# Attention in an encoder block: another order of its units, reciprocals turned by a transpose, later casts, and ScalarE's and VectorE's order fixed by the program

## The chip, the cores and the metric

The kernel runs on one core of a Trainium2 chip. TensorE multiplies, VectorE and GpSimd work elementwise, ScalarE copies, casts and evaluates functions, and SyncE (SP) issues most of the DMAs; ScalarE has a DMA queue of its own. The metric is the device time of one execution in microseconds. The kernel before takes 2630.07, the median of three runs (2628.52 to 2633.43). Units are microseconds throughout.

## The reference

One layer of an encoder block, for 1024 tokens of width 1024, in float32:

```
h      = rmsnorm(x) * (1 + scale1) + shift1          # scale, shift, gate from silu(c) @ w_ada
q, k, v, xBC, z, dt, gates = split(h @ w_in)
q, k   = rope(rmsnorm(q)), rope(rmsnorm(k))          # 16 query heads, 4 key/value heads of 64
attn   = softmax(q k^T / 8) v                        # over all 1024 tokens, per head
ssd    = gated_rmsnorm(scan_fwd(xBC, dt) + scan_bwd(xBC, dt) + D * x, z)
merged = sigmoid(g_a) * (attn @ w_attn_out) + sigmoid(g_s) * (ssd @ w_ssd_out)
x      = x + gate1 * (merged @ w_o)
x      = x + gate2 * (relu(h2 @ w1)^2 @ w2)          # h2: x normed and modulated again
```

The change touches the line `attn` and what is computed beside it: a part of `gates`, and the making ready of `attn` for the product with `w_attn_out`.

## The kernel before

**Products of float32.** Every large product is made of three: an operand is split into a high part (a cast to a 32-bit format that TensorE takes in one pass) and a low part (the operand minus the high part), and the products high·high, high·low and low·high are added in PSUM. `split` does this: ScalarE casts, VectorE or GpSimd (`e_lo=G`) subtracts. `gemm_cm` runs a product whose weights are the stationary operand: per tile `i` of 128 columns and half of the tokens, eight steps of three matmuls. It loads and splits the weights of tile `i + 1` (`load_w`: the DMA, the cast `whi`, the remainder `wlo`) when tile `i` begins.

**Attention** (`attn_stream`) goes through 128 units: 16 heads by 8 tiles of 128 queries. Four units are a block: a head and 512 queries.

- `scores(u)`: four matmuls give a tile `pss` of 128 queries by 1024 keys in PSUM (two such tiles); VectorE takes the negated row maximum `nm` (L914); ScalarE takes the exponential into `pf` in SBUF (two tiles), with the row sums into a column of `zall` (L916).
- `turn(u, hf)`: four transposes (L927) turn half of `pf` into a PSUM tile `pst` (two tiles); ScalarE casts it to `ph`, VectorE subtracts for `pl`. There are three tiles of `ph` and of `pl`; each holds one half of the keys for a block.
- `values(b, hf)`: with `v` as the stationary operand, eight matmuls a half into one PSUM tile `pv`, whose upper rows hold the high part of `v` and whose lower rows the low one. After the second half ScalarE copies one part (`ax`), VectorE adds the other (`av`), GpSimd multiplies by the reciprocals of the row sums (`rz`), and SP writes `av` to DRAM.
- The reciprocals: VectorE takes them (`zi`, 128 queries by 4 tiles); a DMA on SP writes them to DRAM query by query (L941), and another reads them back broadcast over 64 partitions (L943).

The loop over units issues scores of unit u + 2, the first `turn` of unit u, a quarter of the values of the block before, the second `turn`. `values` yields four times, once per four matmuls.

**Beside it** runs `beside()`: first the products of six tiles of `gates` (`gates_stream`, 96 steps; ScalarE copies each result to `ost` and writes it from its own DMA queue), then `load_a`: it splits two tiles of `w_attn_out`, and per pair of heads loads `av` back (`araw`) and splits it at once into `ah` and `al`, the operands of the product after attention.

**What sets the order.** `weave` takes the next step of that stream which is less far along, by costs written into the `yield`s: attention counts 2.72 a unit, 128 × 2.72 + 18 = 366.2 in all, and what runs beside counts 6 × 10.4 + 18 = 80.4, of which a step of gates is 0.65. A step that yields `None` isn't ready. Inside `tc.manual_schedule(engines=...)` the engines named keep the order in which the program issues; the others are ordered by the scheduler, which simulates the kernel and gives each engine the order of that simulation. Before, the set `M2` for attention holds TensorE alone:

```
M2 = {mybir.EngineType.PE}
...
        with tc.manual_schedule(engines=M2):
            weave(tc, (attn_stream(), 128 * 2.72 + L0), (beside(), GATES * 10.4 + 18), lead=LEAD2)
```

On the chip every engine takes its instructions in the order given to it, and waits where an operand or a buffer isn't ready. A DMA's issue is an instruction of the engine whose queue it uses.

Of the kernel before, what the change touches and what calls it, by code (L numbers as in the profile page):

```python
# [9 lines left out]
F32 = mybir.dt.float32  # L10
# [8 lines left out]
P = 128  # L19
S = 1024  # L20
D = 1024
NT = S // P
KT = D // P
NH = 16
NKV = 4
HD = 64
# [6 lines left out]
OFF_Z, OFF_DT, OFF_G = 4608, 6656, 6720  # L33
# [20 lines left out]
SC0, SC1 = 26, 3.5  # L54
GATES = 16 - 2 * len(GPOS)
M3 = {mybir.EngineType.PE}
M2 = {mybir.EngineType.PE}
LEAD3 = 400
BIG = 1.5 * 2.0 ** 15
BAR = 1e30  # L60
# [30 lines left out]
def block(ctx: ExitStack, tc: tile.TileContext, ia, out, upto=99, dbg=None):  # L91
    nc = tc.nc
    V, A, G, T = nc.vector, nc.scalar, nc.gpsimd, nc.tensor
    dma = nc.sync.dma_start
    adma = nc.scalar.dma_start
# [71 lines left out]
    def split(hi, lo, src, e_hi=None, e_lo=None):  # L167
        (e_hi or A.copy)(hi, src)  # L168
        tt(e_lo or V, lo, src, hi.bitcast(F32), ALU.subtract)
# [4 lines left out]
    def act_tiles(name, n):  # L174
        return [[[act.tile([P, 512], F32R, name=f"{name}{p}_{k}_{h}", tag="act", bufs=32)
                  for h in range(2)] for k in range(n)] for p in ("h", "l")]

    def load_w(src, shape=(KT, P), e_lo=None):

        raw = wp.tile([P, *shape], F32, name="wraw", tag="wraw")  # L180
        dma(raw, src)
        hi = wp.tile([P, *shape], F32R, name="whi", tag="whi")
        lo = wp.tile([P, *shape], F32R, name="wlo", tag="wlo")
        split(hi, lo, raw, e_lo=e_lo)
        return hi, lo

    def w_cols(w, c0, k0=0):
        return w[k0 * P:(k0 + KT) * P, c0:c0 + P].rearrange("(k p) c -> p k c", p=P)

    def gemm_cm(ps_pool, tag, wsrcs, ahi, alo, evac, bufs=None, pair=False, then=None, e_lo=None, ws=None):  # L190

        ws = ws or {0: load_w(wsrcs[0], e_lo=e_lo)}
        if then:
            then()
        n = len(wsrcs)
        order = [(i, h) for i in range(n) for h in range(2)]
        if pair:
            order[:4] = [(0, 0), (1, 0), (0, 1), (1, 1)]
        for i, half in order:
            if half == 0 and i + 1 < n and i + 1 not in ws:  # L200
                ws[i + 1] = load_w(wsrcs[i + 1], e_lo=e_lo)
            hi, lo = ws[i]
            if 1:
                ps = ps_pool.tile([P, 512], F32, name=tag, tag=tag, bufs=bufs)
                for k in range(KT):
                    T.matmul(ps, hi[:, k], ahi[k][half], start=k == 0, stop=False)  # L206
                    T.matmul(ps, hi[:, k], alo[k][half], start=False, stop=False)  # L207
                    T.matmul(ps, lo[:, k], ahi[k][half], start=False, stop=k == KT - 1)  # L208
                    yield 0.65
                evac(i, half, ps)  # L210


# [44 lines left out]
    with tc.tile_pool(name="p0", bufs=1) as p0, tc.tile_pool(name="ps0", bufs=1, space=PSUM) as ps0:  # L257
# [57 lines left out]
        late = []  # L315
# [101 lines left out]
    with tc.tile_pool(name="p1", bufs=1, reuse_waits="tile") as p1, \  # L417
# [428 lines left out]
    with tc.tile_pool(name="p3k", bufs=1, reuse_waits="tile") as p3k, \  # L846
# [3 lines left out]
        def gates_stream(pool, psp, i0, i1, bufs=2, e_lo=None):  # L850
            def evac(i, half, ps):
                st = pool.tile([P, 512], F32, name="ost", tag="ost", bufs=2)
                A.copy(st, ps)
                adma(gt_d[i0 + i][:, half * 512:(half + 1) * 512], st)

            yield from gemm_cm(psp, "psg", [w_cols(w_in, OFF_G + i * P) for i in range(i0, i1)], hhi, hlo, evac, bufs=bufs, e_lo=e_lo)

        heads = [0]
        w_ahead = {}

        def load_a():

            hi, lo = act_tiles("a", KT)
            for i in range(2):
                w_ahead[i] = load_w(w_cols(w_ao, i * P), e_lo=G)
            yield 2
            for k in range(KT):
                while heads[0] < 2 * k + 2:
                    yield None
                for half in range(2):  # L870
                    raw = p3.tile([P, 512], F32, name="araw", tag="araw", bufs=2)
                    dma(raw, av_d[k][:, half * 512:(half + 1) * 512])
                    split(hi[k][half], lo[k][half], raw, e_lo=G)
                yield 2
            w_ahead["a"] = hi, lo

# [4 lines left out]
        def attn_stream():  # L881
# [19 lines left out]
            pfs, phs, pls = {}, {}, {}  # L901

            def scores(u):
                h, t = divmod(u, NT)
                q1 = qs[h]
                k1, k2, _ = kv[h // 4]
                ps = ps3.tile([P, S], F32, name="pss", tag="pss", bufs=2)
                ts = slice(t * P, (t + 1) * P)
                for n in range(2):
                    T.matmul(ps[:, n * 512:(n + 1) * 512], q1[:, ts], k1[:, n * 512:(n + 1) * 512], start=True, stop=False)  # L910
                for n in range(2):
                    T.matmul(ps[:, n * 512:(n + 1) * 512], q1[:, ts], k2[:, n * 512:(n + 1) * 512], start=False, stop=True)  # L912
                nm = p3.tile([P, 1], F32, name="nm", tag="nm", bufs=4)
                V.tensor_reduce(out=nm, in_=ps, axis=AX.X, op=ALU.max, negate=True)  # L914
                pfs[u] = p3.tile([P, S], F32, name="pf", tag="pf", bufs=2)
                A.activation(pfs[u], ps, AF.Exp, bias=nm, accum_out=zall[:, u:u + 1])  # L916

# [13 lines left out]
            pvs, rzs = {}, {}  # L931

            def values(b, hf):

                h = b // 2
                v1 = kv[h // 4][2]
                if hf == 0:
                    zi = p3.tile([P, 4], F32, name="zi", tag="zi", bufs=2)
                    V.reciprocal(zi, zall[:, 4 * b:4 * b + 4])
                    row = rz_d[h:h + 1, (b % 2) * 512:(b % 2 + 1) * 512]  # L940
                    dma(row.rearrange("a (t p) -> p (a t)", p=P), zi)  # L941
                    rzs[b] = p3.tile([HD, 512], F32, name="rz", tag="rz", bufs=2)
                    dma(rzs[b], rz_d[h, (b % 2) * 512:(b % 2 + 1) * 512].partition_broadcast(HD))  # L943
                    pvs[b] = ps3.tile([P, 512], F32, name="pv", tag="pv", bufs=1)
                pv, ph, pl = pvs[b], phs.pop((b, hf)), pls.pop((b, hf))
                for k in range(4):
                    kt = hf * 4 + k
                    if kt == 0:
                        T.matmul(pv, v1[:, 0], ph[:, 0], start=True, stop=False)
                    T.matmul(pv[:HD], v1[:, kt, 0:HD], pl[:, k], start=False, stop=False)  # L950
                    if kt:
                        T.matmul(pv, v1[:, kt], ph[:, k], start=False, stop=kt == NT - 1)
                    if k == 1:
                        yield 0.92
                if hf == 1:
                    ax = p3.tile([HD, 512], F32, name="ax", tag="ax", bufs=1)
                    A.copy(ax, pv[HD:])
                    av = p3.tile([HD, 512], F32, name="av", tag="av", bufs=2)
                    tt(V, av, ax, pv[:HD], ALU.add)
                    tt(G, av, av, rzs.pop(b), ALU.mult)  # L960
                    dma(av_d[h // 2][(h % 2) * HD:(h % 2 + 1) * HD, (b % 2) * 512:(b % 2 + 1) * 512], av)
                    heads[0] = (b + 1) // 2
                yield 0.92

            def all_values(b):
                for hf in range(2):
# [27 lines left out]

# [723 lines left out]
```

## Time and profile before

| what | value |
|---|---|
| median of three runs | 2630.07 |
| profiled execution: time, span | 2632.16, 2630.4 |
| mean granted clock of TensorE | 0.973 |
| busy: TensorE, weight loads, VectorE, ScalarE, GpSimd | 2427.9, 1933.0, 1851.1, 1135.3, 1119.9 |
| first and last row maximum of attention | 791.5, 1288.5 |
| last value matmul begins; product after attention begins | 1300.8, 1301.0 |
| TensorE busy in 784 to 1304: transposes, scores, values, gates | 161.6, 173.1, 209.1, 116.7 |
| VectorE there: row maxima, `pl` | 156.6, 166.8 |
| ScalarE there: exponentials, `ph` | 142.7, 143.6 |

The profile is that of one execution; its time is 1.8 above its span and 2.1 above the median. Matmuls overlap in the array, so the sum of their lengths is more than the time they hold TensorE; their distance from start to start is what counts. In a line of the timeline the first numbers are start and length, then engine, line of the code, operation, result `<-` operands and shape; the brackets hold how long the engine had been idle and what ended that. `PEld` is TensorE's weight load, `ACTq` and `SPq` are DMA issues of ScalarE's and SP's queues. L154 and L168 are the lines of the helpers for elementwise operations and casts, so their instructions are told apart by tiles. In the list of waits stand total, times and longest.

### The profile page before, as it was taken

To read this page: it belongs to the slowest core of one execution; us is meant where nothing else is said; L and a number is where in the kernel's file an instruction comes from. 1 tells how busy PE (TensorE), PEld (TensorE's weight loads), DVE (VectorE), ACT (ScalarE), POOL (GpSimd) and SP (SyncE) were. 2 spreads that over 40 slices of the span, in tenths; PEclk is the share of its full clock that TensorE was granted. 3 is DMA by queue.
4 is the path that set the end of the run, shared out by engine and by line. 5 is a ranking of instruction groups with operands and counts; after the bars stand their busy time and mean duration, and the time that the engine had idled before them with its cause. 6 is when DMAs were issued, how large, how long until landed. Compare 5 with 4: busy or idle time off the path is not lost.

```text
span 2630.4 us, 32563 instructions
## 1 busy us (share of the span) xinstructions
PE 2427.9 (92%) x11291; PEld 1933.0 (73%) x11291; DVE 1851.1 (70%) x2203; ACT 1135.3 (43%) x1964; POOL 1119.9 (43%) x828
## 2 busy tenths in 40 slices
PE   5999999999988999887789989999998999899995
PEld 4898777878776677665567767777776888688884
DVE  5756347777776777656567888646569888767889
ACT  5455423444446666665423444444232222264441
POOL 3210117777760111121146656614017765633356
PEclk9999999999999999989999999999899999899998
DMA  7554741333353222221166666466415544764432
GB/s 262 175 156 129 251 145 60 96 106 103 115 180 92 74 61 65 67 69 41 49 205 199 212 201 185 142 212 204 140 61 172 176 152 146 249 192 143 143 96 96
DMA packets 298293, 369.69 MB, mean 141 GB/s; under 512 B 50953, under 2 KB 179569, under 8 KB 298129
## 3 DMA queue, kind: packets, MB, share of 16 engines
q1 hardware_dynamic: 227953, 292.63, 36.2%
q10 hardware_dynamic: 70176, 74.99, 8.6%
q8 instruction: 89, 1.46, 0.3%
q14 instruction: 75, 0.61, 0.1%
HBM read 251.33 MB, written 116.20 MB: 140 GB/s over the span
## 4 chain that ended last, share of the span: by engine, by line
PE 38%; DMA 8%; DVE 6%; issue 3%; POOL 2%; ACT 1%; SPq 0%; DVEq 0%; ACTq 0%; POOLq 0%
PE pp L1323 4%; PE pp L1325 4%; PE pp L1324 4%; PE p L1665 3%; PE p L1666 3%; PE p L1664 3%; DMA rz<-zi 2%; PE psy L1150 2%; PE psg L206 2%; PE pso L1124 2%; DVE o L154 2%; PE psg L207 2%; PE psg L208 2%; DVE ac L154 1%; PE pso L1370 1%
## 5 line engine op out<-in xcount | busy, mean ns | idle before, releaser
L914 DVE TENSOR_REDUCE nm<-pss 128x1 f32<-128x1024 f32 x128 | 156.6, 1224 | 121.3 <-PE pss L912 119.6
L927 PE MATMUL pst<-masks,pf 128*128 128x128 f32 x1024 | 161.6, 281 | 59.7 <-DVE pl L154 59.6
L927 PEld LDWEIGHTS pst<-masks,pf 128*128 128x128 f32 x1024 | 119.8, 143 | 127.8 <-DVE pl L154 51.9
L380 PE MATMUL psq<-twl,hh 128*128 128x400 f32 (+1 forms) x512 | 192.8, 378 | 7.7 <-DVE twl L154 5.9
L1665 PE MATMUL p<-o,o 128*128 128x512 f32 x448 | 179.9, 402 | 19.0 <-DVE o L154 19.0
L154 DVE TENSOR_TENSOR pl<-pst,ph 128x512 fp32r<-128x512 f32 x256 | 166.8, 681 | 43.1 <-ACT ph L168 43.1
L379 PE MATMUL psq<-twh,hh 128*128 128x400 f32 (+1 forms) x512 | 191.7, 380 | 3.4 <-ACT qkvr L512 1.3
L381 PE MATMUL psq<-twh,hl 128*128 128x400 f32 (+1 forms) x512 | 191.5, 376 | 0.5 <-DVE hl L154 0.5
L916 ACT ACTIVATE pf<-pss,nm 128x1024 f32<-128x1024 f32 x128 | 142.7, 1115 | 108.3 <-PE pst L927 103.0
L154 POOL TENSOR_TENSOR av<-av,rz 64x512 f32<-64x512 f32 x32 | 41.0, 1282 | 339.9 <-DVE av L154 332.7
L1664 PE MATMUL p<-o,o 128*128 128x512 f32 x448 | 177.5, 400 | 8.7 <-ACT o L168 6.8
L1666 PE MATMUL p<-o,o 128*128 128x512 f32 x448 | 177.5, 398 | 0.0
L154 POOL TENSOR_TENSOR sl<-sl 128x512 f32<-128x512 f32 x64 | 95.1, 1491 | 175.6 <-DVE o L154 84.3
L713 DVE SCALAR_TENSOR_TENSOR cacc<-pad,cwT,cacc 128x1024 f32<-128x1024 f32 x96 | 159.5, 1691 | 0.4
L168 ACT CAST ph<-pst 128x512 fp32r<-128x512 f32 x256 | 143.6, 586 | 32.9 <-PE pst L927 21.2
L168 ACT CAST o<-ar 128x512 fp32r<-128x512 f32 x112 | 69.8, 624 | 175.8 <-PE p L1666 160.9
L154 DVE TENSOR_TENSOR o<-ar,o 128x512 fp32r<-128x512 f32 x112 | 107.9, 964 | 48.6 <-ACT o L168 48.4
L168 ACT CAST wop<-ws 128x512 fp32r<-128x512 f32 x132 | 81.5, 622 | 130.6 <-PE pp L1325 69.3
L154 POOL TENSOR_TENSOR wop<-ws,wop 128x512 fp32r<-128x512 f32 x68 | 121.5, 1800 | 20.8 <-ACT wop L168 20.6
L1665 PEld LDWEIGHTS p<-o,o 128*128 128x128 f32 x448 | 86.5, 193 | 41.5 <-DVE o L154 23.7
L380 PEld LDWEIGHTS psq<-twl,hh 128*128 128x128 f32 x512 | 98.2, 192 | 20.0 <-DVE twl L154 7.5
L154 DVE TENSOR_TENSOR wop<-r,wop 128x512 fp32r<-128x512 f32 x89 | 97.7, 1098 | 20.5 <-ACT wop L168 20.2
(414 smaller groups left out, 7230.7 us busy)
## 6 DMA issues: line engine op xcount, KB each, us to landing
ar<-r SPq DMA_DIRECT2D x112, 256.0 KB
wada<-in_w_ada_dram SPq DMA_DIRECT2D x48, 512.0 KB
r<-in_w_in_dram SPq DMA_DIRECT2D x34, 512.0 KB
r<-in_w_mlp_dram SPq DMA_DIRECT2D x32, 512.0 KB
r<-as SPq DMA_DIRECT2D x64, 256.0 KB
sl<-in_w_mlp_dram SPq DMA_DIRECT2D x64, 256.0 KB
r<-ro ACTq DMA_DIRECT2D x48, 256.0 KB
xb<-cst ACTq DMA_DIRECT2D x20, 512.0 KB
```

Of the source, the lines that this page charges most:

```text
L154: e.tensor_tensor(out=o, in0=a, in1=b, op=op)
L168: (e_hi or A.copy)(hi, src)
L379: T.matmul(o, hhi[k][half][:, sl], hi[:, k % 2, :n], start=k == 0, stop=False)
L380: T.matmul(o, hhi[k][half][:, sl], lo[:, k % 2, :n], start=False, stop=False)
L381: T.matmul(o, hlo[k][half][:, sl], hi[:, k % 2, :n], start=False, stop=k == KT - 1)
L713: V.scalar_tensor_tensor(out=acc, in0=pad[:, k:k + S], scalar=cwT[:, 24 * k + i:24 * k + i + 1], in1=acc, op0=ALU.mult, op1=ALU.add)
L914: V.tensor_reduce(out=nm, in_=ps, axis=AX.X, op=ALU.max, negate=True)
L916: A.activation(pfs[u], ps, AF.Exp, bias=nm, accum_out=zall[:, u:u + 1])
L927: T.transpose(pt[:, k], pf[:, (hf * 4 + k) * P:(hf * 4 + k + 1) * P], ident)
L1664: T.matmul(pss[t], a[:, 0, sl], b[:, 0], start=k == 0, stop=False)
L1665: T.matmul(pss[t], a[:, 0, sl], b[:, 1], start=False, stop=False)
L1666: T.matmul(pss[t], a[:, 1, sl], b[:, 0], start=False, stop=k == KR - 1)
```

## The change

- `M2` gets ScalarE and VectorE besides TensorE: in attention their instructions keep the program's order, ScalarE's DMA issues with them.
- The exponential leaves `scores` and becomes `weights(u)`. A unit now issues: both `turn`s of unit u with values between them, scores and row maximum of unit u + 2, `sums` in every fourth unit, then the exponential of unit u + 1.
- Values are yielded as 8, 4 and 4 matmuls, so the four units of a block get 8, 4, 4 and none.
- The reciprocals are taken at the start of the block's first unit; `sums` turns them by a transpose on TensorE (into a `pst` tile), ScalarE copies the four rows to `zr` and writes them from its own queue; SP reads them back broadcast as before.
- `gemm_cm` with `late=5` loads the next weights when a tile begins, and splits them after the sixth step of its first half (`raw_w` is the load alone). `load_a` loads both tiles of `w_attn_out` first and splits them later; of `av` it loads both halves of a pair of heads, and splits them when attention is three units further.

```diff
-M2 = {mybir.EngineType.PE}
+M2 = {mybir.EngineType.PE, mybir.EngineType.Activation, mybir.EngineType.DVE}
...
-    def load_w(src, shape=(KT, P), e_lo=None):
-
+    def raw_w(src, shape=(KT, P)):
         raw = wp.tile([P, *shape], F32, name="wraw", tag="wraw")
         dma(raw, src)
+        return raw
+
+    def load_w(src, shape=(KT, P), e_lo=None, raw=None):
+
+        raw = raw_w(src, shape) if raw is None else raw
...
             if half == 0 and i + 1 < n and i + 1 not in ws:
-                ws[i + 1] = load_w(wsrcs[i + 1], e_lo=e_lo)
+                if late is None:
+                    ws[i + 1] = load_w(wsrcs[i + 1], e_lo=e_lo)
+                else:
+                    raws[i + 1] = raw_w(wsrcs[i + 1])
...
                     yield 0.65
+                    if k == late and i + 1 in raws:
+                        ws[i + 1] = load_w(None, e_lo=e_lo, raw=raws.pop(i + 1))
...
+            raws = [raw_w(w_cols(w_ao, i * P)) for i in range(2)]
             for i in range(2):
-                w_ahead[i] = load_w(w_cols(w_ao, i * P), e_lo=G)
-            yield 2
+                yield 2
+                w_ahead[i] = load_w(None, e_lo=G, raw=raws[i])
             for k in range(KT):
                 while heads[0] < 2 * k + 2:
                     yield None
+                raws = [p3.tile([P, 512], F32, name="araw", tag="araw", bufs=2) for half in range(2)]
                 for half in range(2):
-                    raw = p3.tile([P, 512], F32, name="araw", tag="araw", bufs=2)
-                    dma(raw, av_d[k][:, half * 512:(half + 1) * 512])
-                    split(hi[k][half], lo[k][half], raw, e_lo=G)
+                    dma(raws[half], av_d[k][:, half * 512:(half + 1) * 512])
+                u0 = units[0]
+                while units[0] < min(u0 + 3, NH * NT + 3):
+                    yield None
+                for half in range(2):
+                    split(hi[k][half], lo[k][half], raws[half], e_lo=G)
...
                 V.tensor_reduce(out=nm, in_=ps, axis=AX.X, op=ALU.max, negate=True)
+                sms[u] = ps, nm
+
+            def weights(u):
+                ps, nm = sms.pop(u)
                 pfs[u] = p3.tile([P, S], F32, name="pf", tag="pf", bufs=2)
                 A.activation(pfs[u], ps, AF.Exp, bias=nm, accum_out=zall[:, u:u + 1])
...
+            def sums(b):
+
+                pz = ps3.tile([P, 4, P], F32, name="pst", tag="pst", bufs=2)
+                T.transpose(pz[0:4, 0], zis.pop(b), ident)
+                zr = p3.tile([4, P], F32, name="zr", tag="zr", bufs=1)
+                A.copy(zr, pz[0:4, 0])
+                row = rz_d[b // 2, (b % 2) * 512:(b % 2 + 1) * 512]
+                adma(row.rearrange("(t p) -> t p", p=P), zr)
+                rzs[b] = p3.tile([HD, 512], F32, name="rz", tag="rz", bufs=2)
+                dma(rzs[b], row.partition_broadcast(HD))
...
-                    zi = p3.tile([P, 4], F32, name="zi", tag="zi", bufs=2)
-                    V.reciprocal(zi, zall[:, 4 * b:4 * b + 4])
-                    row = rz_d[h:h + 1, (b % 2) * 512:(b % 2 + 1) * 512]
-                    dma(row.rearrange("a (t p) -> p (a t)", p=P), zi)
-                    rzs[b] = p3.tile([HD, 512], F32, name="rz", tag="rz", bufs=2)
-                    dma(rzs[b], rz_d[h, (b % 2) * 512:(b % 2 + 1) * 512].partition_broadcast(HD))
...
-                    if k == 1:
+                    if hf == 1 and k == 1:
                         yield 0.92
...
-                yield 0.92
+                yield 0.92 if hf else 1.84
...
-            scores(0)
-            yield 0.92
-            scores(1)
-            yield 0.92
+            for u in range(2):
+                scores(u)
+                yield 0.92
+            weights(0)
             pvq = iter(())
             for u in range(NU + 4):
+                units[0] = u
                 if u % NT == 4 and 1 < u // NT + 1 < NH:
                     load_head(u // NT + 1)
-                if u + 2 < NU:
-                    scores(u + 2)
-                    yield 0.92
+                b = u // 4 - 1
+                if u % 4 == 0 and u:
+                    zis[b] = p3.tile([P, 4], F32, name="zi", tag="zi", bufs=2)
+                    V.reciprocal(zis[b], zall[:, 4 * b:4 * b + 4])
                 for hf in range(2):
                     if u < NU:
                         turn(u, hf)
                         yield 0.44
                     if hf == 0:
                         c = next(pvq, None)
                         if c:
                             yield c
+                if u + 2 < NU:
+                    scores(u + 2)
+                    yield 0.92
+                if b in zis:
+                    sums(b)
+                if u + 1 < NU:
+                    weights(u + 1)
                 if u % 4 == 3 and u < NU:
                     pvq = all_values(u // 4)
```

More of the change, by code (lines that the diff above doesn't have):

```diff
@@ L188, in w_cols, with gemm_cm @@
         return w[k0 * P:(k0 + KT) * P, c0:c0 + P].rearrange("(k p) c -> p k c", p=P)
-    def gemm_cm(ps_pool, tag, wsrcs, ahi, alo, evac, bufs=None, pair=False, then=None, e_lo=None, ws=None):
+    def gemm_cm(ps_pool, tag, wsrcs, ahi, alo, evac, bufs=None, pair=False, then=None, e_lo=None, ws=None, late=None):
         ws = ws or {0: load_w(wsrcs[0], e_lo=e_lo)}
@@ L194, in gemm_cm @@
             then()
-        n = len(wsrcs)
+        n, raws = len(wsrcs), {}
         order = [(i, h) for i in range(n) for h in range(2)]
@@ L854, in evac @@
                 adma(gt_d[i0 + i][:, half * 512:(half + 1) * 512], st)
-            yield from gemm_cm(psp, "psg", [w_cols(w_in, OFF_G + i * P) for i in range(i0, i1)], hhi, hlo, evac, bufs=bufs, e_lo=e_lo)
-        heads = [0]
+            yield from gemm_cm(psp, "psg", [w_cols(w_in, OFF_G + i * P) for i in range(i0, i1)], hhi, hlo, evac, bufs=bufs, e_lo=e_lo, late=5)
+        heads, units = [0], [0]
         w_ahead = {}
@@ L900, in attn_stream @@
             zall = p3.tile([P, NH * NT], F32, name="zall")
-            pfs, phs, pls = {}, {}, {}
+            sms, pfs, phs, pls = {}, {}, {}, {}
             def scores(u):
@@ L929, in turn @@
                 split(phs[b, hf][:, :, js], pls[b, hf][:, :, js], pt)
-            pvs, rzs = {}, {}
+            pvs, rzs, zis = {}, {}, {}
+            def sums(b):
[7 more added lines that the diff above has]
+                dma(rzs[b], row.partition_broadcast(HD))
             def values(b, hf):
```

## The prediction

> **What bounds the kernel now.** I read the granted clock first, then the windows over attention, the chain of waits, the list of waits, and the timeline for single durations. Of the profiled execution's 2632.16 us (span 2630.4, 1.8 around it), attention is the part from about 790 to 1305; the change is all inside it.
>
> From the windows (PE, PEld, DVE, ACT, POOL, then clock, DMA share, GB/s):
> ```profile
> 950.00:1000.00 50.00, 46.88 (x250) 35.28 (x249) 34.37 (x48) 33.75 (x60) 6.21 (x4) 1.00 0.25 62
> 1100.00:1150.00 50.00, 38.34 (x182) 28.43 (x181) 25.43 (x35) 28.55 (x53) 13.90 (x11) 0.86 0.30 69
> 1200.00:1250.00 50.00, 38.42 (x199) 28.27 (x198) 31.95 (x43) 29.86 (x56) 5.11 (x4) 0.93 0.12 32
> ```
> TensorE is 94% busy while gate products run beside attention, and 77% later. From the chain of waits (start, length, what), a quiet unit and a stall:
> ```profile
> 1214.38 1.22 DVE nm L914
> 1215.60 0.61 DVE pl L154
> 1216.35 0.63 PE pst L927 x4
> 1216.98 0.46 PE pss L910 x2
> 1217.44 0.48 PE pss L912 x2
> 1217.95 0.87 DVE nm L914
> ...
> 1226.36 8.38 DMA rz<-zi
> ...
> 1235.31 4.07 DMA av<-av
> ...
> 1239.42 2.56 DMA araw<-av
> ```
> A **unit** (one head, 128 queries) takes 1217.95 − 1214.38 = 3.57: row maximum on VectorE, remainder `pl`, the transposes that need its PSUM buffer, the next scores, the next maximum. TensorE's own work mostly fits under that loop. The stall is another thing: 2 KB of reciprocals take 8.38 us to be written column by column, SP's queue holds the write of `av` and the loads `araw` behind it, and a cast of `araw` stands in ScalarE's queue ahead of attention's own copies. From the list of waits and the instructions of the scores:
> ```profile
> ACT ah L168 <- DMA araw<-av: 29.8, 6, 7.2
> ```
> ```profile
> L914 DVE TENSOR_REDUCE nm<-pss x128: 1214/1224/1227, 791.5 to 1288.5; 128x1 f32<-128x1024 f32 x128
> ```
> 127 intervals take 497.0, 3.91 a unit; 44 us are above 127 × 3.57, most of it these stalls. At the end attention's loss goes on for 3.30 + 0.84 = 4.1 us of TensorE waiting for the last `ah` and `al`:
> ```profile
> 1300.80 0.19 PEld L206 LDWEIGHTS psg<-ah,whi 128*128 128x128 f32 x1
> ...
> 1309.29 0.50 PE L206 MATMUL psg<-ah,whi 128*128 128x512 f32 x1 [3.30 <-ACT ah L168]
> ...
> 1310.64 0.50 PE L207 MATMUL psg<-al,whi 128*128 128x512 f32 x1 [0.84 <-POOL al L154]
> ```
> So attention ends, in effect, at 1300.8 + 4.1 = 1304.9.
>
> **What is taken away.** The column write goes: reciprocals are turned by a transpose, written as four rows from ScalarE's queue, and SP keeps only the broadcast. `araw` is loaded three units ahead of its casts. With both, the 44 us and the 4.1 us can go. The new row write isn't in the trace: between 2.56 (`araw`) and 8.38 to land; I take 2.56, the shape nearer to whole rows. Write, broadcast and 0.5 of issue then end some 5.6 us after it is issued, about 9.9 into a block of four units, and `av` is multiplied at about 12: hidden. At 8.38 it would be 9 us late: GpSimd, which has only `av` and the remainders of the casts there (5 to 14 us busy in 50), would wait, and the casts, a head or more behind, still not. The row write now stands on ScalarE's queue, behind a write of `gt` once in eight gate steps. Gate weights are cast at the sixth step of a tile's first half and used ten steps later: hidden.
>
> **What the fixed order makes of a unit.** In program order ScalarE does first `ph`, second `ph`, then the exponential of the *next* unit; TensorE does first transposes `pst0`, values (`pv`), `pst1`, scores two units ahead, then the next `pst0`. Before, the exponential of two units ahead ran between the two; now `pst0` of unit u+1 must wait for an exponential that stands behind the second `ph` of unit u. Durations from the timeline:
> ```profile
> 792.75 1.11 ACT L916 ACTIVATE pf<-pss,nm 128x1024 f32<-128x1024 f32 x1 [3.62 <-DVE nm L914]
> ...
> 794.01 0.72 PE L910 MATMUL pss<-k,q 128*128 128x512 f32 x2 [1.65 <-ACT pf L916]
> ...
> 795.93 0.59 ACT L853 COPY ost<-psg 128x512 f32<-128x512 f32 x1 [0.84 <-PE psg L208]
> ...
> 796.55 0.33 ACTq L854 DMA_DIRECT2D gt<-ost  x1
> ...
> 796.97 0.59 ACT L168 CAST ph<-pst 128x512 fp32r<-128x512 f32 x1 [0.45 <-PE pst L927]
> ```
> ```profile
> 967.55 0.60 PE L927 MATMUL pst<-masks,pf 128*128 128x128 f32 x4
> ...
> 968.19 0.59 ACT L168 CAST ph<-pst 128x512 fp32r<-128x512 f32 x1 [0.38 <-PE pst L927]
> ...
> 969.10 0.63 PE L927 MATMUL pst<-masks,pf 128*128 128x128 f32 x4
> ...
> 969.49 0.70 PE L910 MATMUL pss<-k,q 128*128 128x512 f32 x2
> ...
> 970.50 0.60 PE L927 MATMUL pst<-masks,pf 128*128 128x128 f32 x4
> ...
> 971.63 0.40 PE L950 MATMUL pv<-pl,v 128*64 128x512 f32 x1
> ...
> 971.87 0.40 PE L952 MATMUL pv<-ph,v 128*128 128x512 f32 x1
> ```
> ```profile
> 1028.15 0.58 ACT L853 COPY ost<-psg 128x512 f32<-128x512 f32 x1
> 1028.62 1.12 ACT L916 ACTIVATE pf<-pss,nm 128x1024 f32<-128x1024 f32 x1
> ```
> The **wait loop** from `pst1` to the next `pst0`: 0.64 to the copy (967.55 to 968.19), 0.47 from a copy to the exponential behind it (1028.15 to 1028.62), 1.26 from the exponential's start to the TensorE instruction that waits for it (792.75 to 794.01): 2.38. On TensorE four transposes take 0.38, a `pv` 0.23 (971.63 to 971.87), scores 1.01 (969.49 to 970.50).
>
> The values come as 8, 4, 4 and 0 matmuls, in units A, B, C, D of a block:
> B = 0.38 + 0.92 + 2.38 = 3.68. C = 3.73: the copy `ax`, on ScalarE between the two `ph`, can start some 0.2 after the last value and holds the second `ph` for 0.05. D = 0.38 + 2.38, and 0.10 as the second `ph` waits for the first: 2.86.
> A has `sums` besides: `pst1` at 2.22, scores at 2.60, the turning of the reciprocals at 3.61, 0.33 for one transpose and its way, the copy `zr`, its DMA issue, and only then the exponential. `zr` isn't in the trace; the first of these rows is next to it, and the others are what else goes into the stage:
> ```profile
> L1093 ACT COPY cb<-psm x32: 244/265/272, 1352.3 to 1695.6; 128x128 f32<-128x128 f32 x32
> ```
> ```profile
> L927 PE MATMUL pst<-masks,pf 128*128 128x128 f32 x1024 | 161.6, 281 | 59.7 <-DVE pl L154 59.6
> ...
> L957 ACT COPY ax<-pv 64x512 f32<-64x512 f32 x32 | 18.7, 583 | 13.7 <-PE pv L952 12.8
> ...
> L168 ACT CAST ah<-araw 128x512 fp32r<-128x512 f32 x14 | 8.7, 623 | 30.9 <-DMA araw<-av 29.8 <-PE psg L207 1.0
> ...
> L168 ACT CAST whi<-wraw 128x1024 fp32r<-128x1024 f32 x7 | 7.4, 1052 | 2.2 <-PE psc L768 1.4 <-issue 0.8
> ```
> `zr` lies between 0.24 (the fastest `cb`) and 0.59 (the copies of 512 columns); I take 0.26, as its 128 columns are those of `cb`. The DMA issue behind a copy costs nothing when the scheduler puts it later, up to 0.45 when it stands directly behind (copy ends 796.52, next copy 796.97); program order puts it directly behind, so 0.45. Exponential at 3.61 + 0.33 + 0.26 + 0.45 = 4.65; A = 5.91.
> A block is 5.91 + 3.68 + 3.73 + 2.86 = 16.18, 4.05 a unit. VectorE isn't late in it: after `pst1` come 0.64, `ph` 0.59, `pl` 0.68 and the maximum's 1.22, 3.2 with the way between them (3.4 in C, with `av` on VectorE too), and the exponential that needs this maximum starts 2.76 + 1.2 = 3.9 after `pst1` at the earliest. The reciprocal stands ahead of A's first `pl`, which is 1.2 away. Should the cover go, what the maximum is late would add to the loop. The 1.26 rests on one row; it can't be under the exponential's own 1.11, which would take 0.6 off a block.
>
> From the first `pst0` at 794.01: 32 × 16.18 = 517.8, less 4.7 for the first block (no values, no `sums`), plus 3.3 for the last values: 516.4, ending at 1310.4. Against 1304.9 this alone is **+5.5**: the gain of 48 is eaten by the longer loop.
>
> **Gate steps** (three matmuls, 0.70): the weave gives one per 0.65/80.4 × 366.2 = 2.96 of attention's count, 1.09 units. Seven of 96 run ahead of the first scores. One that falls behind `pst1` or the scores hides in the wait (2.38 − 1.39 = 0.99 free); one that falls behind `pst0` or the values delays `pst1`, and in A every one delays the turning or `pst1`. Following the weave's costs gives 33 in A and 9, 10 and 5 such in B, C, D: 57 × 0.70 = **+39.9**. Before, they filled idle time of the 3.57 loop.
> **Copies of ScalarE in between.** `ost` and its issue hold the next instruction for 1.04 (795.93 to 796.97). Behind `pst0` or the values it delays the second `ph` by 0.17 + 1.04 − 0.64 = 0.57 (six of eleven); between second `ph` and exponential it must wait for its matmul (0.38 + 1.01 + 0.70 + 0.17 + 1.04 against 1.11, 2.2, three times); 0.9 once in A, once nothing: **+10.9**. Casts of 1.05 and 0.62 come where the weave's costs put them; of the six of 1.05, four stand whole in front of a second `ph` or an exponential that is due, one for 0.46, one for nothing, 4.7; of seven pairs of 0.62, three fall in D (1.2 each), two in B (0.36), one in C (0.8), one in A (nothing), 5.1: **+9.8**. They stood on ScalarE before too, but there the loop ran through VectorE.
> Sum: 5.5 + 39.9 + 10.9 + 9.8 = **+66**. Profiled 2632.2 gives 2698; the median of the runs, 2630.07, gives **2696**. Nothing after attention hides it: the next products need its last head.
>
> **TensorE's clock.** In A the array rests nearly 2 us. Rows with such rests, and a longer one:
> ```profile
> 1262.55 0.66 PE L927 MATMUL pst<-masks,pf 128*128 128x128 f32 x4 [2.64 <-DVE pl L154]
> ...
> 1178.53 1.12 PE L927 MATMUL pst<-masks,pf 128*128 128x128 f32 x4 [4.91 <-DVE pl L154]
> ```
> After 2.64 the transposes go at full speed, after 4.91 at about half. I take no loss. The Trainium skill (TensorE: Matmul & The Clock Gate, "A second HAM failure mode: psum-queue depth-cycling") says that frequent small rests between groups of matmuls can throttle the clock too; the row after 2.64 doesn't show that, but no stage here has such rests in every block. By that rule the time would be that of the third rival.
>
> **The rivals.**
> *ScalarE's order doesn't bind* (faster). Its place is ScalarE's queue between second `ph` and exponential: if that exponential is never what `pst0` waits for, because the copies ahead of it come early enough, the 3.57 loop stays and the stalls are gone: 128 × 3.57 + 3.3 = 460 against 511, −50, some 5 back for casts: 2585. It decides at 3.97 a unit, gate steps and casts included ((1304.9 − 794.0 − 3.3)/128); I have 4.5. For it: ScalarE and VectorE are only 51 to 69% busy in the windows. Against: the order of `ph`, `ph`, exponential leaves no other way.
> *Half of it hides.* The issue behind `zr` doesn't hold the exponential (−0.45 × 31 = −14) and gate steps in A go under its longer wait (−33 × 0.70 = −23): +29, 2659.
> *The clock falls.* At 0.86, as granted in 1100 to 1150, the loop's TensorE part of 7.7 a block (3.7 values, 3.0 transposes, 1.0 scores) gets 16% longer: 32 × 1.26 = +40, 2736.
> *It does not do what it says*: the scheduler's order stood in this order already, and the rest is hidden: 2630. Against: before, the exponential ran one unit further ahead.
>
> **How the numbers follow.** Chances: forecast 0.61 (its own range 2663 to 2728: the issue at 0 and 1.11 for 1.26, −33; `zr` at 0.59 and all 89 gate steps in the way, +32), half 0.19, clock 0.06, order not binding 0.11, unchanged 0.03. Predicted 2696. A range of 2640 to 2735 takes in the second case, and leaves out the faster one, the unchanged one, half of the clock's and a small tail, 0.2. Runs tell 0.2% (5 us) from no change. Faster 0.11, within 0.2% 0.03, slower 0.86.
>
> **What would show it.** Right: about 4.5 us a unit with gates and 4.05 without; TensorE's longest wait in attention `pst` for the exponential `pf`, where it was `pl`; no wait of `ah` for DMA; the maximum no longer waiting 120 us for scores on the chain; a unit in four near 5.9. Wrong: a unit at 3.6 throughout, exponentials that begin ahead of the second `ph`, or a clock under 1.0 without rests over 4 us.

## The result: 3.5% slower, and the profile after

The changed kernel takes 2722.03 us, the median of four runs (2720.44 to 2726.97), against 2630.70 for the kernel before on the same chip (four runs, 2628.52 to 2633.43). The ratio is 1.035 (95% interval 1.0332 to 1.0368): 91 us lost, where +66 was forecast; the time lies inside the forecast range of 2640 to 2735. The profiled execution took 2726.97, with a span of 2725.2.

The windows over most of attention, first after, then before (columns as in the prediction: PE, PEld, DVE, ACT, POOL, clock, DMA share, GB/s):

```profile
790.00:1240.00 450.00, 358.32 (x1795) 264.14 (x1794) 252.23 (x327) 243.69 (x437) 40.15 (x28) 0.96 0.18 54
```
```profile
790.00:1240.00 450.00, 398.13 (x2090) 297.20 (x2088) 300.65 (x397) 289.28 (x513) 64.19 (x45) 0.98 0.25 67
```

In the same 450 us every engine got less done: 327 instructions of VectorE, not 397. No engine is fuller than before, so the time went into waiting, and a little into the clock. The row maxima and the list of waits after:

```profile
L928 DVE TENSOR_REDUCE nm<-pss x128: 1204/1215/1227, 794.9 to 1382.7; 128x1 f32<-128x1024 f32 x128
```
```profile
PE pst L945 <- ACT pf L934: 128.9, 122, 2.3
...
DVE nm L928 <- PE pss L926: 13.0, 16, 5.9
...
ACT ah L168 <- DMA araw<-av: 9.3, 1, 9.3
```

127 intervals take 587.8, 4.63 a unit (3.91 before). TensorE's transposes wait for the exponential `pf` in 122 of 128 units; before they waited for `pl`. The wait of `ah` for its DMA, 29.8 in six places before, is a single 9.3 at the end of attention. The row maximum waits 13.0 for scores, where it waited some 120. The stalls did go, and a new wait came into nearly every unit. The end of attention on TensorE:

```profile
1394.17 0.39 PE L975 MATMUL pv<-ph,v 128*128 128x512 f32 x1
...
1394.40 0.40 PE L213 MATMUL psg<-ah,whi 128*128 128x512 f32 x1
```

The product after attention follows the last value with no stall. By 1304.9 of the prediction, attention ends 89.5 later. It also began 3.4 later (first row maximum at 794.9, not 791.5), so 86 of the difference arose inside it.

### The profile page after: what moved, and what is told of

Same layout as the page of the kernel before. It is cut to its first block, busy times and chain, and to the rows that moved or that the text cites. A ratio compares the mean times of both kernels' runs of the same rounds, so it can differ in the third digit from the quotient of the medians.

```text
span 2725.2 us, 32476 instructions
## 1 busy us (share of the span) xinstructions
PE 2460.3 (90%) x11323; PEld 1951.7 (72%) x11323; DVE 1857.6 (68%) x2203; ACT 1148.2 (42%) x1996; POOL 1120.8 (41%) x828
## 4 chain that ended last, share of the span: by engine, by line
PE 59%; ACT 11%; DVE 10%; DMA 7%; POOL 6%; issue 5%; ACTq 1%; SPq 1%; DVEq 0%; POOLq 0%
ACT pf L934 5%; PE pst L945 4%; PE pp L1355 4%; PE pp L1357 4%; PE pp L1356 3%; PE psq L389 3%; PE psq L390 3%; PE psq L388 3%; PE p L1697 3%; PE p L1698 3%; PE p L1696 3%; DVE cacc L722 2%; ACT ph L168 2%; PE psg L213 2%; PE pv L973 2%
## 5 line engine op out<-in xcount | busy, mean ns | idle before, releaser
L154 DVE TENSOR_TENSOR pl<-pst,ph 128x512 fp32r<-128x512 f32 x256 | 174.3, 689 | 234.2 <-ACT ph L168 233.9
L154 DVE TENSOR_TENSOR o<-sl,o 128x512 fp32r<-128x512 f32 x112 | 111.9, 999 | 0.1
```

What stands on the lines that cost most here:

```text
L154: e.tensor_tensor(out=o, in0=a, in1=b, op=op)
```

## The experiments

Two theories were open. Theory A: ScalarE's fixed order makes the loss, because the exponential of the next unit stands behind the second `ph`. Rival B: the loss lies in what else changed (the order of the units, the reciprocals on ScalarE's queue, the later casts), or in VectorE's fixed order. Each kernel is an edit of the changed one and was timed beside runs of the kernel before on the same chip (2633.71 for the first four, 2633.88 for the next four, 2632.79 for the last). A unit is the distance from the first to the last row maximum, divided by 127. The groups ran on different chips; a difference between two edited kernels, given below from the medians, comes out up to 3 or 4 larger by the ratios.

| run | edit | median us | ratio to before (95%) | unit | clock, 790 to 1240 |
|---|---|---|---|---|---|
| changed kernel | | 2722.03 | 1.0350 (1.0332 to 1.0368) | 4.63 | 0.96 |
| e1_free_order | neither order fixed | 2618.61 | 0.9944 (0.9928 to 0.9961) | 3.84 | 1.00 |
| e5_scalar_only | ScalarE alone fixed | 2728.53 | 1.0350 (1.0329 to 1.0372) | 4.69 | 0.95 |
| e6_vector_only | VectorE alone fixed | 2612.96 | 0.9918 (0.9899 to 0.9937) | 3.81 | 1.00 |
| e2_exp_between | exponential between the turns | 2627.25 | 0.9977 (0.9968 to 0.9986) | 3.91 | 0.99 |
| e3_sums_behind | exponential ahead of `sums` | 2666.97 | 1.0128 (1.0111 to 1.0145) | 4.19 | 1.00 |
| e4_scores_between | scores and exponential between the turns | 2581.91 | 0.9801 (0.9786 to 0.9816) | 3.50 | 1.00 |
| e8_between_free | the same, ScalarE and VectorE free | 2610.77 | 0.9908 (0.9892 to 0.9924) | 3.75 | 1.00 |
| e7_clock_fill | 12 transposes in a rest | 2706.68 | 1.0280 (1.0261 to 1.0298) | 4.54 | 1.00 |
| e9_fill_two | 2 transposes in a rest | 2714.02 | 1.0314 (1.0297 to 1.0331) | 4.55 | 1.00 |

### e1: the order of ScalarE and VectorE left to the scheduler

```diff
-M2 = {mybir.EngineType.PE, mybir.EngineType.Activation, mybir.EngineType.DVE}
+M2 = {mybir.EngineType.PE}
```

> The changed kernel with one line back: in attention only TensorE keeps the program's order; ScalarE and VectorE are ordered by the scheduler again, which puts the exponential of the next unit between the two copies ph of a unit. Theory A (the loss is ScalarE's fixed order: copy, copy, exponential, then the transposes that wait for it): the wait of the transposes for the exponential goes, a unit falls back to about 3.6 us, the stalls of the kernel before stay gone, so 2570 to 2610 us. Theory B (the loss is the new order of units, values in portions of 8, 4, 4 and reciprocals turned on TensorE, whoever orders the other engines): 2680 us or more.

2618.61: 103 below the changed kernel, and 15 below the kernel before. That is some 9 over the interval of theory A, and 61 under the bound of theory B. So everything in the change but the fixed orders gains about 15, and fixing them costs about 103. Its waits and a stretch of ScalarE:

```profile
PE pst L945 <- DVE pl L154: 51.0, 40, 2.1
...
DVE nm L928 <- PE pss L926: 32.8, 32, 6.0
```
```profile
1004.10 0.59 ACT L168 CAST ph<-pst 128x512 fp32r<-128x512 f32 x1 [0.27 <-PE pst L945]
1004.58 1.12 ACT L934 ACTIVATE pf<-pss,nm 128x1024 f32<-128x1024 f32 x1
1005.68 0.59 ACT L168 CAST ph<-pst 128x512 fp32r<-128x512 f32 x1
```

Left free, ScalarE runs an exponential between the first `ph` (1004.10) and the second (1005.68) of a unit, and TensorE again waits for `pl`, as before. That this wait (51.0) and that for scores (32.8) hold the 9 us by which the interval was missed is likely, but wasn't tried.

### e5 and e6: one engine fixed at a time

```diff
-M2 = {mybir.EngineType.PE, mybir.EngineType.Activation, mybir.EngineType.DVE}
+M2 = {mybir.EngineType.PE, mybir.EngineType.Activation}    # e5
+M2 = {mybir.EngineType.PE, mybir.EngineType.DVE}           # e6
```

> The changed kernel with ScalarE and TensorE in program order, VectorE ordered by the scheduler. Theory A (the loss is ScalarE's fixed order alone): as slow as the changed kernel, 2700 to 2730 us, and the transposes wait for the exponential as long as there. Theory C (both orders together are needed, VectorE's row maximum behind both remainders included): 2650 us or less.

> The changed kernel with VectorE and TensorE in program order, ScalarE ordered by the scheduler. Theory A: the exponential goes ahead of the second copy again, and the time is that of the kernel with both free (2619 us) within 15 us. Theory C: clearly above it, 2650 us or more.

The wait of the transposes for the exponential, in e5 and then in e6:

```profile
PE pst L945 <- ACT pf L934: 129.0, 118, 2.3
```
```profile
PE pst L945 <- ACT pf L934: 37.6, 47, 2.0
```

With ScalarE alone fixed, time and wait are those of the changed kernel; with VectorE alone fixed, the time is within 6 of e1. The loss is ScalarE's order alone, and rival B falls.

### e2: the exponential moved between the two copies

```diff
@@ the loop over units
                         c = next(pvq, None)
                         if c:
                             yield c
+                        if u + 1 < NU:
+                            weights(u + 1)
...
                 if b in zis:
                     sums(b)
-                if u + 1 < NU:
-                    weights(u + 1)
```

> The changed kernel, all three engines in program order, with one instruction moved: the exponential of unit u+1 stands between the two turns of unit u, ahead of the second copy ph, and not behind scores and sums. Theory A: the loop of 2.38 us from the second transposes to the next first ones no longer has the exponential in it; what is left is copy, remainder, row maximum, exponential, copy (0.59+0.05+0.65+1.22+0.05+1.1 = 3.65 us a unit), some 0.7 more in the first unit of a block: about 2610 to 2640 us. Theory B (gate steps, casts and the turning cost what they cost wherever the exponential stands): 2690 us or more.

2627.25: one instruction's place, with all three engines still fixed, gives back 95 of the 103. One of ScalarE's longer waits is now this:

```profile
ACT pf L934 <- DVE nm L928: 38.7, 37, 5.2
```

The exponential now comes early enough to wait for its row maximum, which VectorE takes behind the second `pl` of the unit before, as the scores are issued last in a unit.

### e3: the exponential ahead of the reciprocals' copy

```diff
-                if b in zis:
-                    sums(b)
                 if u + 1 < NU:
                     weights(u + 1)
+                if b in zis:
+                    sums(b)
```

> The changed kernel with the turning of the reciprocals (transpose, copy zr, DMA issue) issued behind the exponential of the next unit and not ahead of it. By the sum of the prediction the first unit of a block falls from 5.9 (measured about 6.0 without a gate step) to about 4.6 to 4.7: 31 blocks by 1.3 us, some 40 us, 2680 us; more if the clock, which falls behind that wait in some blocks, stays up. Rival: ScalarE only waits elsewhere (the copy zr then stands ahead of the next copy ph): 10 us or less, 2712 to 2722 us.

2666.97, 55 below the changed kernel. By the units of both traces, from one unit's first transposes to the next's, 35 of it is the shorter path (a block's first unit falls from 5.86 to 4.73, 31 times), about 12 the clock, which stays at 1.00 (worked out with e7 below), and the rest, about 9, gate steps and copies: of two gate steps in a block's first unit one now hides (5.43 with two, 5.42 with one). In a block's first unit, ScalarE goes from the second `ph` straight to the exponential, and `zr` and its DMA issue follow it:

```profile
1220.09 1.12 ACT L934 ACTIVATE pf<-pss,nm 128x1024 f32<-128x1024 f32 x1
...
1221.19 0.24 ACT L956 COPY zr<-pst 4x128 f32<-4x128 f32 x1
...
1221.35 0.66 PE L945 MATMUL pst<-masks,pf 128*128 128x128 f32 x4 [0.74 <-ACT pf L934]
1221.45 0.25 ACTq L958 DMA_DIRECT2D rz<-zr  x1
```

TensorE's rest there is 0.74, where it is 1.87 in the changed kernel (its row stands below, with the reciprocals).

### e4 and e8: scores and exponential between the turns

```diff
-                for hf in range(2):
-                    if u < NU:
-                        turn(u, hf)
-                        yield 0.44
-                    if hf == 0:
-                        c = next(pvq, None)
-                        if c:
-                            yield c
+                if u < NU:
+                    turn(u, 0)
+                    yield 0.44
                 if u + 2 < NU:
                     scores(u + 2)
                     yield 0.92
-                if b in zis:
-                    sums(b)
                 if u + 1 < NU:
                     weights(u + 1)
+                if b in zis:
+                    sums(b)
+                c = next(pvq, None)
+                if c:
+                    yield c
+                if u < NU:
+                    turn(u, 1)
+                    yield 0.44
```

e8 has the same, and `M2 = {mybir.EngineType.PE}`.

> The changed kernel with a unit in another program order: first turn, scores of u+2, exponential of u+1, sums, values, second turn; all three engines fixed. The exponential starts behind the first copy ph, and the row maximum stands between the two remainders, so no engine's order closes a loop longer than TensorE's own 2.65 us of a unit, 3.2 with gate steps: attention takes 128 by 3.25 to 3.5 us and the whole 2530 to 2570 us by theory A (a fixed order costs only by what it puts in the loop). Rival (any fixed order loses against the scheduler's, since it can't react to which copy is due): not under 2600 us.

> The kernel with scores between the turns (2582 us with all three engines fixed), with ScalarE and VectorE ordered by the scheduler. If a fixed order helps once the program's order is a good one: the scheduler, which takes other durations than the chip's, is slower, 2595 to 2620 us. If the order of units is all that counts and the scheduler finds the rest: 2575 to 2590 us.

e4 takes 2581.91 (2578.04 to 2582.89), 2% below the kernel before, though 12 over its interval. Its unit of 3.50 is the upper end of what was expected (3.25 to 3.5); 127 units that are 0.41 shorter than before make 52, which is the whole of the gain, so the interval of the time was set too low for that of the unit. Its window, its row maxima and what is left of the two waits:

```profile
790.00:1240.00 450.00, 427.13 (x2330) 328.83 (x2329) 328.45 (x442) 321.66 (x601) 67.80 (x48) 1.00 0.23 70
```
```profile
L928 DVE TENSOR_REDUCE nm<-pss x128: 1204/1215/1225, 791.9 to 1236.5; 128x1 f32<-128x1024 f32 x128
```
```profile
PE pst L945 <- ACT pf L934: 12.0, 27, 1.6
DVE nm L928 <- PE pss L926: 11.3, 12, 5.9
```

TensorE is busy for 427 of 450 at full clock; two waits that held up the others have shrunk to 12 each. With the same program and the scheduler's order (e8), 29 us more are needed, and the old waits are back:

```profile
PE pst L945 <- DVE pl L154: 53.2, 52, 1.6
...
DVE nm L928 <- PE pss L926: 31.3, 61, 9.1
```

So fixing the order is neither good nor bad by itself: with this program it gains 29, with the changed kernel's it costs 103. Fixing the order of the kernel before wasn't tried.

### e7 and e9: TensorE's clock

```diff
                 pt = ps3.tile([P, 4, P], F32, name="pst", tag="pst", bufs=2)
+                if hf == 0 and u % 4 == 1 and u > 4:
+                    for k in range(12):                        # e9: range(2)
+                        T.transpose(pt[:, k % 4], ident, ident)
```

The transposes of a unit matrix go into a tile that the turn overwrites afterwards. They only fill TensorE's rest at the end of a block's first unit.

> The changed kernel with 12 more transposes of the unit matrix ahead of the first turn of each second unit of a block; they write the tile that the turn then overwrites, and fall into the rest of some 2 us in which TensorE waits for the exponential behind the turned reciprocals. Nothing is taken away. Theory (the part of the loss that the prediction missed is TensorE's clock, granted 0.96 in attention against 1.00 with the turning behind the exponential): the granted clock goes to 1.00, and the time falls by 10 to 17 us, to 2705 to 2712 us, although TensorE has 31 by 1.1 us more work. Rival (the lower clock only fills waits): 2719 us or more.

> The changed kernel with 2 transposes of the unit matrix, not 12, ahead of the first turn in each block's second unit (about 0.25 of TensorE's time, within the rest of 1.87). In the changed kernel the granted clock halves for stretches of 3.41, and nearly always behind a stretch of 3.41 in which TensorE had been busy for 1.54 (0.45 of it) or less; stretches with 1.68 (0.49) are followed by full speed. Theory A: what counts is the busy share of such a stretch, with the limit between 0.45 and 0.49. Two transposes lift it to about 0.52: the clock in 790 to 1240 is 0.99 to 1.00, and the time is that of the kernel with 12, 2702 to 2712. Rival B: any rest of 1.3 or more in every block lowers the clock in proportion to its length. Then the clock stays at 0.96 to 0.97, and the time is 2716 to 2723.

The window over attention in e7, then in e9:

```profile
790.00:1240.00 450.00, 385.63 (x2120) 289.47 (x2118) 261.80 (x340) 251.58 (x452) 38.66 (x27) 1.00 0.17 51
```
```profile
790.00:1240.00 450.00, 359.06 (x1878) 263.13 (x1876) 261.26 (x340) 251.37 (x452) 38.66 (x27) 1.00 0.17 52
```

More work on TensorE makes the kernel 15 us faster (2706.68), and the clock goes from 0.96 to 1.00. With two transposes the profiled execution does the same (2706.15), but the other three took 2713.88 to 2717.6, with a mean clock over the whole program of 0.974 to 0.975, against 0.977 in the profiled one. The median, 2714.02, lies between the intervals of theory A and rival B. What this settles stands in the next section, with the clock.

## Why the prediction was right, and where it was off

**The sign and the mechanism: right.** The loop from `pst1` through the second `ph` and the exponential to the next `pst0` was named as the new bound, and e1, e2, e5 and e6 show that this order, and nothing else in the change, makes the loss. A block's units are called A to D, as in the prediction. Unit C, without a gate step, in the timeline after:

```profile
1241.32 0.66 PE L945 MATMUL pst<-masks,pf 128*128 128x128 f32 x4 [0.18 <-ACT pf L934]
...
1241.73 0.48 PE L973 MATMUL pv<-pl,v 128*64 128x512 f32 x1
...
1242.04 0.40 PE L975 MATMUL pv<-ph,v 128*128 128x512 f32 x1
...
1242.74 0.60 PE L945 MATMUL pst<-masks,pf 128*128 128x128 f32 x4
1242.94 0.58 ACT L980 COPY ax<-pv 64x512 f32<-64x512 f32 x1 [0.34 <-PE pv L975]
...
1243.55 0.59 ACT L168 CAST ph<-pst 128x512 fp32r<-128x512 f32 x1
...
1244.03 1.12 ACT L934 ACTIVATE pf<-pss,nm 128x1024 f32<-128x1024 f32 x1
...
1245.29 1.09 PE L945 MATMUL pst<-masks,pf 128*128 128x128 f32 x8 [0.33 <-ACT pf L934]
```

From the second `ph` to the exponential 0.48 (forecast 0.47), from there to the next transposes 1.26 (forecast 1.26, which had rested on one row). From `pst0` to `pst1`, though, 1.42, not 1.30: the four transposes hold TensorE for 0.41 (1241.32 to 1241.73) and the first value matmul for 0.31 (to 1242.04), where 0.38 and 0.23 were put in. And `ax` holds the second `ph` until 0.81 after `pst1`, not 0.69. C is 3.97.

**The units.** The medians of units without a gate step or a cast are A 5.86, B 3.80, C 3.97, D 2.93 (forecast 5.91, 3.68, 3.73, 2.86): 16.56 a block, not 16.18, which is +12 over 32 blocks. Up to the last one with a gate step a unit is 4.72 on average, after it 4.37, with casts still in the way (forecast 4.5 with gate steps and 4.05 without). The chain shows the transposes of D, of the next A (which holds one gate step) and of B:

```profile
1245.29 0.67 PE pst L945 x4
...
1248.22 0.66 PE pst L945 x4
...
1254.77 0.66 PE pst L945 x4
...
1260.36 0.66 PE pst L945 x4
```

D takes 2.93; A 6.55, which is 5.86 and a gate step of 0.69: "in A every one delays" was right (A with two steps has a median of 7.24). B, with 5.59, is 1.09 above 3.80 and its own gate step of 0.70: more on that below.

**The reciprocals.** How A ends, in the timeline:

```profile
1252.93 0.25 ACT L956 COPY zr<-pst 4x128 f32<-4x128 f32 x1 [0.46 <-PE pst L954]
...
1253.22 0.25 ACTq L958 DMA_DIRECT2D rz<-zr  x1
1253.51 1.11 ACT L934 ACTIVATE pf<-pss,nm 128x1024 f32<-128x1024 f32 x1 [0.32 <-DVE pl L154]
1254.38 0.46 SPq L960 DMA_DIRECT2D rz<-rz  x1
...
1254.77 0.66 PE L945 MATMUL pst<-masks,pf 128*128 128x128 f32 x4 [1.87 <-ACT pf L934]
```

`zr` takes 0.25 (forecast 0.26), the exponential starts 0.58 after `zr`'s start (forecast 0.71, the issue at 0.45): it begins at 1253.51, where the issue ends, and not at the end of `pl`, 1253.20, which the bracket names. SP's broadcast, which reads what was written, is issued 1.16 after the write's issue: the row write takes less than the 2.56 that were put in for it, and far less than the column write's 8.38. It was hidden, as forecast, and the waits that it had caused are gone. The second rival, by which the issue doesn't hold the exponential, falls by these rows and by the gate steps in A, each of which costs its 0.69; e3, which takes the turning, `zr` and its issue out of the path, gains 55.

**Gate steps, `ost` and casts.** Forecast 39.9 + 10.9 + 9.8 = 60.6. Over the quiet units, those with a gate step alone took 36.9 more, those with a cast or an `ost` 25.8: 62.7 together (blocks after the first). That looks right, but the clock's loss is in it. In e7, whose quiet units are those of the changed kernel to 0.01 and whose clock is 1.00, the same units take 52.3 more than quiet ones. So the forecast was 8 too high here, and the clock covers that up.

**The clock: the step that failed.** "I take no loss" rested on one row: after a rest of 2.64 the transposes at 1262.55 went at full speed. That row was read too early. What follows it in the trace of before, and the windows over the two stretches of 3.41 there:

```profile
1262.55 0.66 PE L927 MATMUL pst<-masks,pf 128*128 128x128 f32 x4 [2.64 <-DVE pl L154]
...
1263.32 0.63 PE L952 MATMUL pv<-ph,v 128*128 128x512 f32 x1
...
1264.60 1.05 PE L927 MATMUL pst<-masks,pf 128*128 128x128 f32 x4
```
```profile
1259.80:1263.21 3.41, 0.77 (x6) 0.67 (x6) 1.41 (x2) 2.54 (x5) 1.27 (x1) 1.00 0.09 32
1263.21:1266.62 3.41, 3.41 (x11) 2.59 (x11) 1.67 (x4) 1.51 (x3) 0.00 (x0) 0.50 0.07 1
```

At 1263.21, just as those transposes end, the clock halves, for 3.41. The same after the change, around the rest of 1.87 at the end of an A; and for comparison a stretch that was a little busier:

```profile
1252.71:1256.12 3.41, 1.54 (x10) 1.17 (x9) 1.66 (x3) 2.04 (x4) 0.00 (x0) 1.00 0.07 25
1256.12:1259.54 3.42, 3.42 (x12) 2.63 (x11) 0.96 (x2) 0.93 (x2) 0.00 (x0) 0.50 0.04 14
...
1102.53:1105.94 3.41, 1.68 (x10) 1.09 (x8) 1.82 (x2) 1.96 (x4) 0.00 (x0) 1.00 0.00 1
1105.94:1109.35 3.41, 3.27 (x19) 2.72 (x19) 1.28 (x2) 1.88 (x4) 0.00 (x0) 1.00 0.10 38
```

The columns are those of the windows above. A stretch in which TensorE was busy for 1.54 of 3.41 is followed by one at half clock, one with 1.68 by one at full clock. That is the unit B of 5.59: 3.42 of it ran at half clock. In e7 the same unit, with the same gate step, takes 4.51:

```profile
1240.13 0.66 PE pst L948 x4
...
1244.64 0.66 PE pst L948 x4
```

Between 800 and 1390, 14 stretches ran at half clock. In the stretch ahead of them TensorE had been busy for 1.54 (0.45) or less 13 times and for 1.63 (0.48) once; one stretch with 1.54 was followed by full clock, and so were all others with 1.56 or more. So it isn't the length of a rest alone that decides, but where it falls. Of the 37 rests of 1.7 or more in that time, 15 lie whole within one stretch, and 12 of these are followed by half clock; 22 are cut in two by the end of a stretch, and one is. In e5, the kernel with the same rests, it is 18 of 21 and none of 15. That fits with 11 of the 31 units B being hit, and not all.

The cost follows from e7: there B takes 4.13 on average, where it is 4.51 in the changed kernel, and A, C and D are the same to 0.01. 32 × 0.38 is 12 us within attention, of the 15 (18 by the ratios) by which e7 is faster. The third rival (the clock at 0.86, 2736) had the right mechanism and too low a clock: 0.96. And the prediction's own sign of being wrong, "a clock under 1.0 without rests over 4 us", came out: the longest rest between 800 and 1390 is 2.26.

e9 shows that the limit isn't sharp. There a stretch busy for 1.67 (0.49), as much as in some that full clock follows in the changed kernel, is followed by half clock:

```profile
1162.84:1166.25 3.41, 1.67 (x8) 0.82 (x6) 1.82 (x2) 1.93 (x5) 0.00 (x0) 1.00 0.21 77
1166.25:1169.66 3.41, 3.26 (x12) 2.68 (x13) 0.69 (x1) 0.68 (x3) 0.00 (x0) 0.50 0.10 38
```

The Trainium skill (TensorE: Matmul & The Clock Gate, "What's actually happening") says that the clock is judged in free-running windows of 3413 ns; the traces agree, with stretches of 3.41. The rule weighed in the prediction (the Trainium skill, TensorE: Matmul & The Clock Gate, "A second HAM failure mode: psum-queue depth-cycling"), that frequent small rests throttle the clock, was nearer to this kernel than the row that was set against it.

**The sum.** Attention was to end at 1310.4 + 60.6 = 1371.0 and ends at 1394.4, 23 later. By the traces, +12 of that is the clock, which was put at nothing, and +12 the quiet unit (4.14, not 4.05). The start adds 3.5: the 794.01 of the sum is a score matmul in the trace before, and the changed kernel's first transposes begin at 797.46. The first block adds 3 (14.5 for 11.5, with one unit partly at half clock) and the last values 1; gate steps and copies take 8 back. Without the clock's loss the kernel is 73 above the kernel before (e7, 2706.68 against 2633.88), where 66 was forecast. That this is so near is in part luck, as the quiet unit and the gate steps were off in opposite directions. Another 5 of the profiled execution's 95 arose after attention; their cause stays open.

**The rivals otherwise.** "ScalarE's order doesn't bind" was put at 2585, and falls for this program; e4 shows what it would have needed, another program order, and then takes 2582. "It does not do what it says" falls with e1.

## What to carry to other kernels

Fixing an engine's order makes the program text the schedule: before doing so, follow each engine's queue through one unit and ask what stands ahead of the instruction on which the next unit waits. Here the place of one exponential behind a copy that needn't precede it cost about 95 us (e2), and scores and exponential moved between the two turns made the same fixing worth 29 us (e4 against e8). When a rest appears in every block, look at the clock over the few microseconds *behind* the first instruction after it, not at that instruction alone.

## What the runs showed of the hardware that wasn't expected

- In the changed kernel TensorE's clock halves for 3.41 after a stretch of 3.41 in which it was busy for 1.54 or less (13 of 14 such stretches); rests of 1.87 are enough where they fall into one stretch. The limit isn't sharp: in e9 a stretch busy for 0.49 was followed by half clock, and its executions, which should all have lain above the limit by the changed kernel's trace, took 2706 to 2718. The place of the stretches against the program wasn't controlled, so their share in that spread stays open.
- Adding work made a kernel faster: 12 transposes a block, 15 us less (e7).
- A DMA issue that stands behind a short copy on ScalarE's queue costs little by itself: `zr`, its issue and the way to the exponential take 0.58 together, in every block but the first.
